# A one-column constant tile widened by 64 bytes in a two-layer hybrid attention kernel

## The chip, the cores and the metric

The kernel runs on one core of a Trainium2 chip. The metric is device microseconds of one execution. Before the change the median of 3 runs is 918.7 us, with runs from 918.14 to 919.21 us.

## The reference

A decoder trunk of two layers on x of 256 tokens by 1024 features, all in float32. Each layer has three sublayers, each followed by a layer norm of (alpha x + f(x)):

```
for l in range(DEPTH):
    y = hybrid_mixer(x, ...)                 # sparse, latent and forgetting attention, gated and merged
    x = layer_norm(DN_ALPHA * x + y, ...)
    y = memory_cross_attention(x, mem, ...)  # 4 heads into mem (256 rows)
    x = layer_norm(DN_ALPHA * x + y, ...)
    y = jnp.square(jax.nn.relu(x @ mlp_w_up[l])) @ mlp_w_down[l]
    x = layer_norm(DN_ALPHA * x + y, ...)
```

The weights are some 140 MB of float32, read once; nearly all the arithmetic is dense products of x, or of something made from x, with them.

## The kernel before

**Products in three passes.** Every dense product is made of float32r matmuls. A value v is split into hi = v rounded by ScalarE's write to float32r and lo = v - hi by VectorE. A product a b is then hi hi + lo hi + hi lo, accumulated in one PSUM bank. This is `mm3` (L317 to L325); its one matmul call is L322, so nearly all of TensorE's work carries that line, and groups are told apart by the tile names. In a row `mm<-xhi,whi` the first name after the arrow is the moving operand, the second the stationary one that the weight load brings in.

**Two shapes of product.** `f_tile` (L327) makes features on the partitions: the weights are stationary (128x128) and x moves (256 columns), 8 k-tiles by 3 passes, 24 matmuls per unit of weights. `t_chunk` (L579) makes tokens on the partitions: x is stationary and the weights move, mostly 512 columns at a time. In a layer, 65 units go through `f_tile` with x moving (misc, fq, fk, nq, ncv, nk, gmf, gn, up). With x stationary `t_chunk` takes 4 units each of t1, t2 and ut (48 matmuls of 512 columns each), and xq (48 of 256 columns). Other products have no x in them: the merged heads (`ofm`, `on`), the latent rows (`chi`, `clo`), the memory (`phi`, `plo` in the cross attention), the compressed windows (`xc`), the merged rows `mg` and the hidden layer `hh`, `hl`.

**The weight stream.** All weights lie in HBM in the order of use, as units of [128, 1024] float32. `load_to` (L242) has SyncE load each into one of 5 `raw` buffers; `split_piece` (L254) makes `whi`, `wlo` (6 buffers each) or, for t1, ut and mem, `phi`, `plo` in pages. `pump` (L272) is called from `tick` after a microsecond of products and splits a few units ahead.

**SBUF.** `run` (L1127) opens the pools in a fixed order: consts, small, raw, wp, pg (12 pages of 4096 bytes, 6 halves of 2048 bytes, both per partition), sp, pp. Each tile takes its bytes per partition, rounded up to 32, and the next begins behind it. `first_loads` (L356) allocates, in the order of the consts pool, `xhi` and `xlo` (8192 bytes each), then `mhalf` (one column of -0.5, for the power -1/2 on GpSimd), then `cst` and `ropek`. What comes later lies behind `mhalf`. Where the built program puts them, in bytes of a partition:

```
tile                       begins at    modulo 128
xhi, xlo                   16512, 24704      0
mhalf                      32896             0
cst                        32928            32
biasq, xtok                36576, 45792     96
raw (first of 5)           61248            64
whi, wlo (first of 6)      81728, 106304    64
halves (first of 6)        130880           64
pages (first of 12)        143168           64
sp and pp tiles            from 192320      64
```

The tiles of raw, whi, wlo, the halves, the pages, sp and pp lie multiples of 1024 bytes apart, and the slices that the dense products read begin at multiples of 512 bytes within their tile, so all of these have one remainder modulo 128.

Of the kernel before, what the change touches and what calls it, by code (L numbers as in the profile page):

```python
# [10 lines left out]
F32 = mybir.dt.float32  # L11
# [4 lines left out]
PSUM = bass.MemoryType.PSUM  # L16

S = 256
D = 1024
L = 2  # L20
P = 128
# [4 lines left out]
ROOT = 32.0  # of D  # L26
SPL = 512
# [14 lines left out]
RW0 = 271  # L42
# [24 lines left out]
def f_units(w, cols):  # L67
    """[K, n*128] columns -> n units of [128, K//128 * 128]."""
    k = w.shape[0] // P
    out = []  # L70
    for c in cols:
        sub = w[:, c] if not isinstance(c, slice) else w[:, c]
        out.append(sub.reshape(k, P, P).transpose(1, 0, 2).reshape(P, k * P))
    return out


def t_units(w, per):
    """[K, n] -> units of `per` k-tiles, [128, per * n]."""
    k = w.shape[0] // P
    a = w.reshape(k // per, per, P, w.shape[1]).transpose(0, 2, 1, 3)  # L80
    return [u.reshape(P, -1) for u in a]
# [106 lines left out]
class Halves:  # L188
    """Two tiles of four k-tiles, indexed as one."""
# [12 lines left out]
class Side:  # L202
    """Steps in order, each with the ticks to wait since the one before."""
# [26 lines left out]
class Kernel:  # L230
# [10 lines left out]
    # -- weights: load ahead, split each into hi + lo of 12 bits --  # L241
    def load_to(self, u):  # L242
        """Loads of the units up to u."""
        src = self.a["wst"]
        while self.next_load <= min(u, len(self.units) - 1):
            t = self.raw.tile([P, 1024], F32, name="raw", tag="raw")
            n = 512 if self.next_load == 0 else 1024
            for c in range(0, 1024, n):
                self.nc.sync.dma_start(t[:, c:c + n], bass.AP(
                    tensor=src.tensor, offset=src.offset + self.next_load * P * 1024 + c, ap=[[1024, P], [1, n]]))  # L250
            self.raws[self.next_load] = t
            self.next_load += 1

    def split_piece(self):  # L254
        """Splits the next SPL columns of the stream."""
        u, c = divmod(self.next_piece, 1024 // SPL)
        self.next_piece += 1
        self.load_to(u)
        if c == 0:
            if self.paged(u):  # L260
                self.halves[u] = (self.page([P, 1024], F32R, "phi"), self.page([P, 1024], F32R, "plo"))
            else:
                self.halves[u] = tuple(self.wp.tile([P, 1024], F32R, name=n, tag=n) for n in ("whi", "wlo"))
        sl = (slice(None), slice(c * SPL, c * SPL + SPL))
        hi, lo = self.halves[u]
        self.nc.scalar.activation(hi[sl], self.raws[u][sl], AF.Copy)  # L266
        self.nc.vector.tensor_sub(lo[sl], self.raws[u][sl], r(hi[sl]))  # L267
# [4 lines left out]
    def pump(self):  # L272
        """One piece ahead of use, as far as the buffers reach."""
        u = self.next_piece // (1024 // SPL)
        if u >= len(self.units):
            return
        used = self.offs[self.gi]
        ahead = sum(not self.paged(v) for v in range(used, u))
        if u - used < AHEAD_PAGED and (self.paged(u) or ahead < AHEAD):
            self.split_piece()  # L280
        self.load_to(self.next_piece // (1024 // SPL) + LOADS)
# [16 lines left out]
    # -- chains of steps that are emitted between the dense products --  # L298
    def tick(self, us):
        """After `us` of dense products on the tensor engine."""  # L300
        self.work += us
        while self.work >= TICK:
            self.work -= TICK
            for q in self.side:
                q.tick()
            self.pump()
# [8 lines left out]
    # -- products in three passes --  # L315
    def mm3(self, out, pairs, first=True, last=True):
        """pairs: ((lhs hi, lhs lo), (rhs hi, rhs lo)) accumulated in out."""  # L317
        mm = self.nc.tensor.matmul
        n = len(pairs)
        for ps, (i, j) in enumerate(((0, 0), (1, 0), (0, 1))):  # L320
            for k, (a, b) in enumerate(pairs):
                mm(out, a[i], b[j], start=first and ps == 0 and k == 0,  # L322
                   stop=last and ps == 2 and k == n - 1)
            self.tick(n * out.shape[-1] / 2400)
# [11 lines left out]
    def to_hilo(self, hi, lo, src, scale=None):  # L336
        """hi + lo = src * scale"""
        nc = self.nc
        if scale is None:
            nc.scalar.activation(hi, src, AF.Copy)  # L340
            nc.vector.tensor_sub(lo, src, r(hi))  # L341
        else:
            nc.scalar.activation(hi, src, AF.Copy, scale=scale)
            nc.vector.scalar_tensor_tensor(lo, src, scale, r(hi), op0=OP.mult, op1=OP.subtract)
# [10 lines left out]
    # -- set-up --  # L355
    def first_loads(self):  # L356
        nc, c, a = self.nc, self.consts, self.a
        # products of zeros, so that the tensor engine's clock is up when the first data come
        zero = self.half([P, 512], mybir.dt.bfloat16, "zero")
        nc.vector.memset(zero, 0.0)  # L360
        ps = self.bank("S", [P, 512])
# [14 lines left out]
        self.mhalf = c.tile([P, 1], F32, name="mhalf")  # L376
# [10 lines left out]
    def bias_tables(self):  # L387
        nc, c, a = self.nc, self.consts, self.a
# [5 lines left out]
        # the bias by distance, from -RW0 on; later read in skewed rows  # L394
        rs = self.page([8, RW], F32, "rs")
        for i in range(2):
            ps = self.bank("S", [P, 512])
# [4 lines left out]
    def bias_tables2(self):  # L402
# [3 lines left out]
        for q in range(4):  # L406
            # row p holds distances from p - RW0 on; keys run against them
# [34 lines left out]
    # -- x <- LayerNorm(alpha x + f); then its transposed halves --  # L442
    def ln_part(self, tb, i, ac, square=True):
        """z = alpha x + f for half a row, its sum, its mean square about the mean of the first half."""
# [20 lines left out]
    def layer_norm(self, tb, gb, final=False):  # L465
        """Adds the rest as steps."""
# [5 lines left out]
        def stats():  # L472
            z = st["z"] = self.page([P, D], F32, "lnz")
            # the variance is the mean square about the first half's mean less the square of the means' difference
# [29 lines left out]
    # -- attention over 64-wide heads, in pairs on the partitions --  # L504
    def probs(self, p_ap, s_ap, bias, sums, nmax):
        """p = exp(s + bias - max), its row sums"""
# [7 lines left out]
    def attend(self, qk, bias, v, kbs, done, apart=False):  # L514
        """Four heads with their own keys and values, as two chains of steps (logits to probabilities, the rest).
        qk(ps, h): the logits of head h; v(kb, h): values; done(o, pairs): o in PSUM, per pair of heads 128 columns;
        apart: one pair at a time."""
        nc = self.nc
        nk = P * len(kbs)
        # heads of one half of the partitions share a bank; sums in the order (parity, pair)  # L520
# [46 lines left out]
    def chain(self, units, q=0, wait=1.0):  # L567
        """Steps of units: the first chain of a unit between those of the second of the unit before."""
# [9 lines left out]
    def t_chunk(self, us, acc, x, per, n, tbs=(0, 1), tb_outer=True):  # L578
        """Token rows of x @ w for token blocks; unit u holds `per` k-tiles of n columns."""  # L579
# [8 lines left out]
    def mixer(self, l):  # L588
        nc, s = self.nc, self.small
        x = (self.xhi, self.xlo)  # L590
# [50 lines left out]
        # per head; row 64: 1 beside the keys' sums of -log f, row 65: the queries' sums of log f beside 1  # L641
# [8 lines left out]
        # gates and forget logits in token rows  # L650
# [8 lines left out]
        # -log sigmoid(z) = max(-z, 0) + log1p(exp(-|z|)), log1p(u) = 2 atanh(u / (2 + u))  # L659
# [21 lines left out]
        # selected / window values: [block, branch, group, hi | lo]  # L681
# [6 lines left out]
        # cumulative sums of -log f, turned into rows: [(block, head), token], + and -  # L688
# [75 lines left out]
        # windows of the compressed branch: [(parity, d), k-tile, keys | values, hi | lo, group, window]  # L764
# [21 lines left out]
        # keys of (selected, window): hi in both halves, lo beside the hi of q  # L786
# [42 lines left out]
        def cmp_keys():  # L829
            # in two halves like those above: hi (both halves), lo; per head a block of 16 of 64 columns  # L830
# [8 lines left out]
        def cmp_values():  # L839
            # block-diagonal over the heads of a group  # L840
# [172 lines left out]
    def cross(self, l):  # L1013
# [6 lines left out]
        # queries by token rows, so that the first block starts early; then transposed  # L1020
# [6 lines left out]
        for tb in range(2):  # L1027
# [21 lines left out]
            # weighted sums wait for the values  # L1049
# [31 lines left out]
    def mlp(self, l):  # L1081
# [3 lines left out]
        # the first four tiles of the hidden layer by token rows, one token block at a time  # L1085
# [86 lines left out]
```

## Time and profile before

| | |
|---|---|
| median of 3 runs | 918.7 us (918.14 to 919.21) |
| profiled execution: span from first to last instruction | 916.6 us |
| median run less that span (what lies around it; the profile gives no other time for its own execution) | 2.1 us |
| TensorE busy | 894.2 us, 98% of the span, 6062 matmuls |
| VectorE, ScalarE, GpSimd busy | 639.3, 540.3, 53.3 us |
| granted TensorE clock, mean | 0.997 of full |
| read from HBM | 158.68 MB, 174 GB/s over the span |

The page of a profile lists busy time by engine, the span in 40 slices, the DMA queues, the chain of work that ended last, and the costliest groups of instructions with the mean length of one. The length of one matmul covers its whole way through the array, and matmuls overlap: what one costs in a row of equal ones is the distance from a start to the next start, which the view of instructions in order of time gives. There equal neighbours are merged into one row, with the start of the first and their number.

### The profile page before, as it was taken

How to read it: one execution, taken by the hardware profiler on the slowest of the kernel's cores; microseconds unless marked ns; L12 is line 12 of the kernel's file. 1: busy time of each engine (PE TensorE's matmuls, PEld its weight loads, DVE VectorE, ACT ScalarE, POOL GpSimd, SP SyncE). 2: the span in 40 equal slices, each digit the busy share in tenths (PEclk: the TensorE clock that was granted, in tenths of full speed). 3: DMA queues.
4: the chain of work that ended last, by engine and by line, in shares of the span. 5: the costliest groups of instructions: out<-in, count | busy, mean ns of one | idle time of the engine just before them, and what ended most of it. 6: DMA issues, size and time to landing. Idle time of an engine off the chain costs nothing.

```text
span 916.6 us, 16139 instructions
## 1 busy us (share of the span) xinstructions
PE 894.2 (98%) x6062; PEld 800.2 (87%) x6062; DVE 639.3 (70%) x1401; ACT 540.3 (59%) x1167; POOL 53.3 (6%) x114
## 2 busy tenths in 40 slices
PE   8999999999999999999999999999999999999996
PEld 6899898998877999999888999889978689999995
DVE  5888787759886555555776988776678855555554
ACT  6777856556674555445655876665566644445551
POOL 1000000000211000000130000000021300000002
PEclk9999999999999999999999999999999999999998
DMA  8855544547463666656645445444567536665631
GB/s 324 264 178 156 199 141 139 159 139 274 145 224 128 194 184 185 186 195 193 207 129 170 142 137 183 139 138 138 143 249 232 173 132 194 188 186 189 190 104 46
DMA packets 46539, 160.80 MB, mean 175 GB/s; under 512 B 5941, under 2 KB 7381, under 8 KB 46334
## 3 DMA queue, kind: packets, MB, share of 16 engines
q1 hardware_dynamic: 46462, 159.78, 54.2%
q8 instruction: 47, 0.77, 0.3%
q14 instruction: 30, 0.25, 0.1%
HBM read 158.68 MB, written 1.07 MB: 174 GB/s over the span
## 4 chain that ended last, share of the span: by engine, by line
PE 87%; DVE 4%; POOL 3%; ACT 2%; issue 1%; DMA 1%; SPq 0%; DVEq 0%; POOLq 0%; ACTq 0%
PE mm L322 52%; PE S L322 13%; PE O L322 10%; PE S L903 1%; PE T L919 1%; POOL mv L476 1%; PE S L744 1%; PE S L1041 1%; DVE xtok L486 1%; PE O L944 1%; DVE xtok L450 1%; DVE wlo L267 1%; DVE xlo L341 1%; PE T L551 1%; PE O L561 1%
## 5 line engine op out<-in xcount | busy, mean ns | idle before, releaser
L267 DVE TENSOR_TENSOR wlo<-raw,whi 128x512 fp32r<-128x512 f32 x524 | 341.3, 687 | 119.0 <-ACT whi L266 115.2
L266 ACT ACTIVATE whi<-raw 128x512 fp32r<-128x512 f32 x524 | 302.9, 625 | 151.9 <-issue 98.4
L322 PE MATMUL mm<-xhi,whi 128*128 128x256 f32 x1024 | 144.9, 283 | 0.0
L322 PE MATMUL mm<-xlo,whi 128*128 128x256 f32 x1024 | 144.1, 282 | 0.0
L322 PE MATMUL mm<-xhi,wlo 128*128 128x256 f32 x1024 | 142.9, 281 | 0.0
L322 PEld LDWEIGHTS mm<-xhi,whi 128*128 128x128 f32 x1024 | 131.4, 188 | 5.4 <-issue 2.9
L322 PEld LDWEIGHTS mm<-xlo,whi 128*128 128x128 f32 x1024 | 130.2, 188 | 2.5 <-issue 0.5
L322 PEld LDWEIGHTS mm<-xhi,wlo 128*128 128x128 f32 x1024 | 130.0, 188 | 2.4 <-issue 1.3
L459 POOL TENSOR_SCALAR mv<-mv 128x1 f32<-128x1 f32 x36 | 9.1, 265 | 745.6 <-DVE xtok L450 744.6
L512 ACT ACTIVATE P<-sb,nm 128x128 f32<-128x128 f32 (+1 forms) x96 | 42.8, 447 | 16.0 <-DVE nm L510 15.8
L322 PE MATMUL S<-whi,hh 128*128 128x512 f32 x128 | 50.4, 394 | 0.0
L322 PE MATMUL S<-wlo,hh 128*128 128x512 f32 x128 | 50.1, 391 | 0.0
L322 PE MATMUL O<-whi,hh 128*128 128x512 f32 x128 | 50.0, 391 | 0.0
L322 PE MATMUL O<-wlo,hh 128*128 128x512 f32 x128 | 49.9, 390 | 0.0
L322 PE MATMUL O<-whi,hl 128*128 128x512 f32 x128 | 49.8, 389 | 0.0
L322 PE MATMUL S<-whi,hl 128*128 128x512 f32 x128 | 49.7, 389 | 0.0
L1116 DVE TENSOR_TENSOR tg<-tg 128x512 f32<-128x512 f32 x28 | 19.4, 693 | 38.7 <-ACT tg L1115 38.7
L1115 ACT ACTIVATE tg<-mm 128x512 f32<-128x512 f32 x28 | 16.7, 598 | 43.5 <-PE mm L322 43.5
L461 ACT ACTIVATE lnsq<-xtok,mv 128x512 f32<-128x512 f32 x24 | 17.3, 723 | 27.9 <-POOL mv L459 15.3
L267 DVE TENSOR_TENSOR plo<-raw,phi 128x512 fp32r<-128x512 f32 x40 | 25.9, 689 | 4.9 <-ACT phi L266 4.7
L322 PEld LDWEIGHTS S<-wlo,hh 128*128 128x128 f32 x128 | 24.0, 188 | 5.6
L322 PEld LDWEIGHTS O<-whi,hl 128*128 128x128 f32 x128 | 24.0, 188 | 5.1
(304 smaller groups left out, 1438.0 us busy)
## 6 DMA issues: line engine op xcount, KB each, us to landing
raw<-in_wst_dram SPq DMA_DIRECT2D x281, 512.0 KB, 3.7
lng<-in_lng_dram SPq DMA_DIRECT2D x6, 512.0 KB, 5.5
lnb<-in_lnb_dram SPq DMA_DIRECT2D x6, 512.0 KB, 5.8
wskew<-bias_scratch SPq DMA_DIRECT2D x4, 400.0 KB, 6.7
xt<-in_xT_dram SPq DMA_DIRECT2D x4, 256.0 KB, 4.2
xtok<-in_xtok_dram SPq DMA_DIRECT2D x1, 1024.0 KB, 5.6
out_dram<-xtok SPq DMA_DIRECT2D x4, 256.0 KB
raw<-in_wst_dram SPq DMA_DIRECT2D x2, 256.0 KB, 5.1
```

The costliest lines, as they stand in the source:

```text
L266: self.nc.scalar.activation(hi[sl], self.raws[u][sl], AF.Copy)
L267: self.nc.vector.tensor_sub(lo[sl], self.raws[u][sl], r(hi[sl]))
L322: mm(out, a[i], b[j], start=first and ps == 0 and k == 0, stop=last and ps == 2 and k == n - 1)
L341: nc.vector.tensor_sub(lo, src, r(hi))
L450: nc.vector.scalar_tensor_tensor(xs, xs, ALPHA, ac, op0=OP.mult, op1=OP.add, accum_out=mv[:, i:i + 1])
L461: nc.scalar.activation(sq, xs, AF.Square, bias=mv[:, 4:5], scale=1.0 / ROOT, accum_out=mv[:, 2 + i:3 + i])
L476: nc.gpsimd.tensor_scalar(col[9], col[8], col[8], col[7], op0=OP.mult, op1=OP.subtract)
L486: nc.vector.scalar_tensor_tensor(x[:, c], st["z"][:, c], col[11], gb[1][:, c], op0=OP.mult, op1=OP.add)
L512: nc.scalar.activation(p_ap, t[:, :n], AF.Exp, bias=nmax, scale=-1.0, accum_out=sums)
L551: nc.tensor.transpose(tp[:, h, :], pts[h % 2][:, h // 2, kb * P:(kb + 1) * P], self.ident)
L1115: nc.scalar.activation(t, ps, AF.Relu)
L1116: nc.vector.tensor_mul(t, t, t)
```

## The change

`mhalf` is allocated as 17 columns of which the first is used, 68 bytes for 4. With the rounding to 32 bytes, everything behind it in SBUF begins 64 bytes later. `xhi` and `xlo` lie ahead of it and stay. Comments are taken out elsewhere (their lines stay, blank), and a blank line is added here, so lines from 377 on count one higher. No instruction is added, removed or moved on any engine.

```diff
@@ -373,7 +373,8 @@
             if i % 2 == 0:
                 for _ in range(2 * 1024 // SPL):
                     self.split_piece()
-        self.mhalf = c.tile([P, 1], F32, name="mhalf")
+
+        self.mhalf = c.tile([P, 17], F32, name="mhalf")[:, 0:1]
         nc.vector.memset(self.mhalf, -0.5)
         self.load_to(6)
         self.cst = c.tile([P, K_END], F32, name="cst")
```

The built program's positions with the change, modulo 128: `xhi`, `xlo`, `mhalf` 0 (as before); `cst` 96; `biasq`, `xtok` 32; raw, whi, wlo, halves, pages, sp and pp tiles 0. Modulo 256, x begins at 128 in both; raw, whi, wlo and the pages at 64 before and at 128 with the change. Modulo 512, x begins at 128; whi, wlo and the pages at 320 before and at 384 with the change.

## Rows read from the trace of the kernel before

**Rows 1.** The page: busy time and instructions; granted clock of the 40 slices.

```profile
PE 894.2 (98%) x6062; PEld 800.2 (87%) x6062; DVE 639.3 (70%) x1401; ACT 540.3 (59%) x1167; POOL 53.3 (6%) x114
...
PEclk9999999999999999999999999999999999999998
```

**Rows 2.** The page: chain that ended last, shares of the span by engine.

```profile
PE 87%; DVE 4%; POOL 3%; ACT 2%; issue 1%; DMA 1%; SPq 0%; DVEq 0%; POOLq 0%; ACTq 0%
```

**Rows 3.** Groups by line and shape, TensorE: name, shape, count, busy us, mean ns.

```profile
L322 PE MATMUL mm<-xhi,whi 128*128 128x256 f32 x1024 | 144.9, 283 | 0.0
...
L322 PE MATMUL mm<-onhi,whi 128*128 128x256 f32 x64 | 10.3, 283 | 0.0
...
L322 PE MATMUL mm<-whi,xhi 128*128 128x512 f32 x32 | 10.3, 402 | 0.0
```

**Rows 4.** TensorE in order of time, 196.5 to 216 us: start, length, group.

```profile
198.39 1.10 PE L322 MATMUL mm<-xhi,wlo 128*128 128x256 f32 x8
199.34 1.10 PE L322 MATMUL mm<-xlo,whi 128*128 128x256 f32 x8
...
202.16 1.10 PE L322 MATMUL mm<-xlo,whi 128*128 128x256 f32 x8
...
203.59 0.64 PE L322 MATMUL mm<-onhi,wlo 128*128 128x256 f32 x4
...
214.15 0.64 PE L322 MATMUL mm<-onlo,whi 128*128 128x256 f32 x4
```

**Rows 5.** The same view, 476 to 500 us.

```profile
477.31 1.07 PE L322 MATMUL mm<-xhi,wlo 128*128 128x256 f32 x8
...
486.38 1.07 PE L322 MATMUL mm<-xlo,whi 128*128 128x256 f32 x8
...
488.65 0.63 PE L322 MATMUL mm<-wlo,xhi 128*128 128x512 f32 x2
...
498.45 0.62 PE L322 MATMUL mm<-wlo,xhi 128*128 128x512 f32 x2
```

**Rows 6.** The same view, 440 to 476 us: hidden layer by the weights of the down product.

```profile
446.09 0.39 PE L322 MATMUL S<-whi,hh 128*128 128x512 f32 x1
...
453.12 0.39 PE L322 MATMUL O<-whi,hl 128*128 128x512 f32 x1
```

**Rows 7.** The same view, 171 to 181 us: among steps of attention.

```profile
172.12 0.40 PE L322 MATMUL mm<-ofmhi,wlo 128*128 128x256 f32 x2
...
173.07 0.41 PE L322 MATMUL mm<-ofmlo,whi 128*128 128x256 f32 x2
...
175.16 1.07 PE L322 MATMUL mm<-xhi,wlo 128*128 128x256 f32 x8
176.07 1.07 PE L322 MATMUL mm<-xlo,whi 128*128 128x256 f32 x8
```

**Rows 8.** The same view, 69 to 73 and 632 to 637 us: first and last row of eight lasting 1.07 us.

```profile
71.58 1.07 PE L322 MATMUL mm<-xlo,whi 128*128 128x256 f32 x8
...
633.58 1.07 PE L322 MATMUL mm<-xhi,wlo 128*128 128x256 f32 x8
```

**Rows 9.** The same view, 245.9 to 253 us: queries of the cross attention, x stationary.

```profile
246.12 0.62 PE L322 MATMUL mm<-whi,xhi 128*128 128x256 f32 x4
...
248.84 0.62 PE L322 MATMUL mm<-whi,xhi 128*128 128x256 f32 x4
```

**Rows 10.** Groups by line and shape, ScalarE: the rounding that makes the upper halves.

```profile
L266 ACT ACTIVATE whi<-raw 128x512 fp32r<-128x512 f32 x524 | 302.9, 625 | 151.9 <-issue 98.4 <-PE mm L322 25.8 <-ACT hh L340 10.1
...
L340 ACT ACTIVATE xhi<-xt 128x512 fp32r<-128x512 f32 x4 | 2.4, 619 | 1.5 <-DMA xt<-in_xT_dram 1.5
```

**Rows 11.** Groups by line and shape, VectorE: the subtraction that makes the lower halves.

```profile
L267 DVE TENSOR_TENSOR wlo<-raw,whi 128x512 fp32r<-128x512 f32 x524 | 341.3, 687 | 119.0 <-ACT whi L266 115.2
...
L341 DVE TENSOR_TENSOR xlo<-xt,xhi 128x512 fp32r<-128x512 f32 x4 | 2.7, 686 | 1.4 <-ACT xhi L340 1.4
```

**Rows 12.** DMA issues: tile, count, KB each, median us from issue to landing.

```profile
raw<-in_wst_dram SPq DMA_DIRECT2D x281, 512.0 KB, 3.7
```

**Rows 13.** Chain that ended last, in order of time: its two longest DMA pieces.

```profile
2.10 6.19 DMA raw<-in_wst_dram
...
86.36 6.14 DMA wskew<-bias_scratch
```

## The prediction

> **What bounds the kernel now.** First the page's busy times: TensorE is busy for 894.2 of 916.6 us, VectorE for 70% and ScalarE for 59% [rows 1]. Then the chain that ended last: 87% of it is TensorE's, 1% DMA [rows 2]. [...] So the time is the sum of what the matmuls cost in a row, and a change that moves no instruction counts by what it does to that distance from start to start.
>
> The reader is then to see that the distance is not one number. [...] The groups by shape hide the difference (x and `on` as the moving operand both show a mean of 283 ns, the length of the whole way through the array [rows 3]). The view in order of time has it:
> - x moving, 256 columns: from 198.39 to 202.16 us are 32 starts, 117.8 ns each, 0.943 us per eight [rows 4]. That is the common, long step.
> - `on` moving, 256 columns, right behind it and with the same kind of stationary weights: from 203.59 to 214.15 us are 88 starts, 120.0 ns each [rows 4].
> - x moving again at 477.31 to 486.38 us: 80 starts, 113.4 ns each, 0.907 us per eight [rows 5]. A row of eight at this short step lasts 1.07 us, at the long one 1.10 us; I counted 41 short ones among the 390 rows of eight, the first at 71.58 us and the last at 633.58 us [rows 8].
> - x stationary, 256 columns: 246.12 to 248.84 us, 24 starts, 113.3 ns each [rows 9].
> - x stationary, 512 columns: 488.65 to 498.45 us, 42 starts, 233.3 ns each [rows 5].
> - no x, 512 columns: 446.09 to 453.12 us, 31 starts, 226.8 ns each [rows 6].
>
> Shape, dtype, line and pass structure are the same within each width. What goes with the step is whether x is one of the two operands. With x in the pair (one operand at 0 modulo 128, the other at 64) the step is 113 or 118 ns, whichever of the two x is, and 233 ns for 512 columns. Without x (both at 64) it is 120 and 227 ns. I read this as: the step depends on how the two operands' starts lie to each other, because moving the odd one from one operand to the other changes less than taking it away.
>
> **The change part by part.** Everything behind `mhalf` moves by 64 bytes together, so the places of weights, pages, halves and small tiles to each other stay. Only the places of `xhi` and `xlo` to the rest change: x and its partner now have equal remainders, as `on` and its weights have now. The terms:
>
> 1. *x moving, 256 columns.* 130 units (65 in each of 2 layers) by 24 matmuls are 3120, or 390 runs of eight. 82 units (misc, fq, fk, gn, up), 246 runs, stand in long rows: they go from 0.943 to 8 x 120.0 = 0.960 us, +0.017 each, +4.2 us. The other 48 units (nq, ncv, nk, gmf), 144 runs, are cut up by steps of attention. There `ofm` without x goes from 172.12 to 173.07 us in 8 starts, 118.8 ns each [rows 7], so a run goes from 0.943 to 0.950, +0.007, +1.0 us. The 41 runs with the short step have 0.036 us more to lose, +1.5 us. Together +6.7 us. The bounds: 0, if all run as those among attention, and +8.1 us, if all come to 120.0.
> 2. *x stationary, 512 columns.* t1, t2 and ut of 2 layers are 288 matmuls. From 233.3 to 226.8 ns is -6.5 ns each, -1.9 us. Bounds 0 and -1.9.
> 3. *x stationary, 256 columns.* xq, 96 matmuls, from 113.3 to 120.0 ns, +0.6 us. Bounds 0 and +0.6.
> 4. *Products without x*, some 740 of 256 and 1000 of 512 columns: both operands move alike, so I take 0. The short step bounds it at -4.9 us for the former (740 by 6.6 ns); that is priced in the first rival, and the other side in the last.
> 5. *ScalarE and VectorE.* Writing to x (at 0) where reading from 64 takes 619 and 686 ns, against 625 and 687 ns when both are at 64 [rows 10, 11]. Even 6 ns on the 564 pieces of the splits are 3 us of engines that wait for TensorE for longer than that; 0. That cover is gone only where TensorE waits for a split, and the chain has 4% of VectorE and 2% of ScalarE [rows 2]: 1% of 6% of 917 us is 0.5 us either way.
> 6. *DMA.* No row here has a load that lands at 0 modulo 128. A unit takes 3.7 us to land [rows 12] and five buffers stand ahead of use; on the chain are two long pieces, 6.19 and 6.14 us [rows 13]. A tenth more or less on both is 1.2 us either way; I take 0, since the order and sizes of all loads stay.
> 7. *`mhalf` itself.* The memset and the powers on GpSimd read and write the same one column; the chain's 3% of GpSimd stays.
>
> Sum: 6.7 - 1.9 + 0.6 = +5.4 us. On the profiled execution the span goes from 916.6 to 922.0 us. The median of the runs stands 2.1 us above that span, so I expect 924.1 us, and say **924 us**. With the bounds of the terms the forecast's own range is 921 to 928 us.
>
> [...]
>
> **The rivals.**
>
> *Faster: the next pairing is the free one.* The mechanism is that the two streams of reads meet at certain distances only, and that the distance x to weights repeats over more than 128 bytes. `on` and its weights lie 0 apart modulo 512; x and its weights will lie 256 apart, which no row shows. Then x's runs would all take the short step, 0.907 us: 349 runs by -0.036 are -12.6 us, with term 2 -14.5 us: **904 us**. If instead each operand's own start counted, the products without x would gain their 4.9 us too, 899 us. It decides wherever f_tile runs: 82 units would show rows of 1.07 us. For it: the short step exists with x and never in the long row of `on`. Against it: x as moving and x as stationary operand lie 64 and 192 apart modulo 256 and 320 and 192 modulo 512, and the pair shows the same short step, so the pattern looks like one of 128 bytes.
>
> *No change.* The step would come from something that goes with x but not from its address: its tile is 8192 bytes, and its chains are 8 long where those of `on` are 4. For it: the 113 and 118 ns steps both occur at unchanged addresses [rows 5, 7], so the address is not all. The mixed products, whose x-less rows are as long as x's, speak against it [rows 4, 6]. [...] **918.7 us**, 917 to 920.
>
> *Slower by more.* Products without x lose their good step of 512 columns: 1000 by 6.5 ns are +6.5 us, and term 2 gives nothing back, +1.9: **932 us**. Nothing in the trace asks for it.
>
> **How the numbers follow.** A difference under about 0.2% (1.8 us) can't be told from none. The forecast has a chance of 0.52, slower by more 0.04, no change 0.13, faster 0.31 (the distances 256 apart are seen in no row, so this stays large). Slower by over 0.2% then has 0.56, within 0.2% 0.13, faster 0.31. The range must reach from the forecast over no change into the faster case until 2 in 10 are out: up to 928, leaving out the slower rival, and down to 903, which takes in x's short step at 904 but not the larger gain at 899. Cases of both signs hold the most of it; the likeliest one's own range is 921 to 928.
>
> **What would show it.** In the changed kernel's view in order of time: rows of eight with x moving 0.960 us apart in the mlp and the gn stretch, pairs of t2 0.454 us apart instead of 0.467, `on` and the hidden layer as before, and fewer rows of 1.07 us. If rows with x come at 0.907 us, the first rival is right; if they stay at 0.943, the second. If t2 goes to 0.454 but x moving does not go to 0.960, places to each other count, but not as I read them. Any change in the idle time of ScalarE or VectorE before the splits larger than 3 us would make terms 5 and 6 wrong.

## The result and the profile after

The changed kernel takes 924.6 us (median of 4 runs, 924.43 to 925.72), against 918.45 us for the kernel before in the same comparison (4 runs): 1.0067 times as long, interval 1.0055 to 1.0078. Its profiled execution has a span of 923.9 us, 7.3 more than before.

The page shows first where the change does not act. Instruction counts, VectorE, ScalarE, GpSimd and the clock's slices are as in [rows 1], and the chain's shares are those of [rows 2] but for a point of ScalarE. Only TensorE's busy time, for matmuls and for weight loads, has grown.

```profile
PE 900.3 (97%) x6062; PEld 809.1 (88%) x6062; DVE 639.7 (69%) x1401; ACT 539.9 (58%) x1167; POOL 53.3 (6%) x114
...
PEclk9999999999999999999999999999999999999998
...
PE 87%; DVE 4%; ACT 3%; POOL 3%; DMA 1%; issue 1%; SPq 0%; DVEq 0%; POOLq 0%; ACTq 0%
```

TensorE in order of time after the change (start, length, group), the stretch of [rows 4]:

```profile
198.91 1.12 PE L322 MATMUL mm<-xlo,whi 128*128 128x256 f32 x8
199.87 1.12 PE L322 MATMUL mm<-xhi,whi 128*128 128x256 f32 x8
...
204.67 1.12 PE L322 MATMUL mm<-xlo,whi 128*128 128x256 f32 x8
...
206.11 0.64 PE L322 MATMUL mm<-onhi,wlo 128*128 128x256 f32 x4
...
216.67 0.64 PE L322 MATMUL mm<-onlo,whi 128*128 128x256 f32 x4
```

With x moving, 48 starts take 204.67 - 198.91 = 5.76 us, 120.0 ns each, where they took 117.8. `on` moving has 88 starts in 10.56 us, 120.0 ns as before. The stretch of [rows 5] had the short step:

```profile
481.06 1.12 PE L322 MATMUL mm<-xhi,wlo 128*128 128x256 f32 x8
...
490.65 1.12 PE L322 MATMUL mm<-xlo,whi 128*128 128x256 f32 x8
...
492.97 0.62 PE L322 MATMUL mm<-wlo,xhi 128*128 128x512 f32 x2
...
502.50 0.62 PE L322 MATMUL mm<-wlo,xhi 128*128 128x512 f32 x2
```

Now 80 starts take 9.59 us, 119.9 ns each, where they took 113.4. A row of eight lasts 1.12 us: the rows of 1.07 us [rows 8] are gone. The t2 product goes the other way: 42 starts in 9.53 us, 226.9 ns where it was 233.3. The two smaller stretches, xq [rows 9] and the hidden layer without x [rows 6], in the same view:

```profile
249.12 0.64 PE L322 MATMUL mm<-whi,xlo 128*128 128x256 f32 x4
...
251.52 0.64 PE L322 MATMUL mm<-whi,xhi 128*128 128x256 f32 x4
```

```profile
449.95 0.39 PE L322 MATMUL S<-whi,hh 128*128 128x512 f32 x1
...
456.75 0.39 PE L322 MATMUL O<-whi,hh 128*128 128x512 f32 x1
```

xq takes 2.40 us for 20 starts, 120.0 ns (113.3 before); the hidden layer 6.80 us for 30, 226.7 ns, as before. The groups by shape hide all of this again: the mean length of one matmul has moved by 3 ns [rows 3], and the two engines that make the splits are as in [rows 10, 11].

```profile
L267 DVE TENSOR_TENSOR wlo<-raw,whi 128x512 fp32r<-128x512 f32 x524 | 341.2, 686 | 121.4 <-ACT whi L266 118.0
L266 ACT ACTIVATE whi<-raw 128x512 fp32r<-128x512 f32 x524 | 302.5, 624 | 154.7 <-issue 99.7 <-PE mm L322 27.0 <-ACT hh L340 9.9
L322 PE MATMUL mm<-xhi,whi 128*128 128x256 f32 x1024 | 147.0, 286 | 0.0
```

For the whole execution I summed, over all matmuls of a class, the distance from each start to the next one on TensorE, whatever that is. A distance up to 150 ns (260 ns for 512 columns) counts for the mean step; longer ones are joints, where TensorE went over to other work or waited.

| class | matmuls | sum before, us | sum after, us | difference | step before, ns | step after, ns |
|---|---|---|---|---|---|---|
| x moving, 256 columns | 3120 | 377.3 | 385.0 | +7.6 | 117.4 | 119.8 |
| x stationary, 512 columns | 288 | 73.9 | 73.0 | -1.0 | 233.3 | 227.8 |
| x stationary, 256 columns (xq) | 96 | 11.6 | 12.0 | +0.4 | 114.7 | 119.5 |
| no x, 256 columns | 724 | 92.8 | 92.8 | 0.0 | 119.7 | 119.6 |
| no x, 512 columns, most by `hh` or `hl`, the rest by `mg` and the heads of the cross attention | 1007 | 236.6 | 236.3 | -0.3 | 228.0 | 227.8 |

Together +6.9 of the span's +7.3 us (differences and their total are from unrounded sums). The classes with x carry it; those without hardly move.

### The profile page after: what moved, and what is told of

It is laid out like the page before. It is cut to its first block, busy times and chain, and to the rows that moved or that the text cites. A ratio compares the mean times of both kernels' runs of the same rounds, so it can differ in the third digit from the quotient of the medians.

```text
span 923.9 us, 16139 instructions
## 1 busy us (share of the span) xinstructions
PE 900.3 (97%) x6062; PEld 809.1 (88%) x6062; DVE 639.7 (69%) x1401; ACT 539.9 (58%) x1167; POOL 53.3 (6%) x114
## 3 DMA queue, kind: packets, MB, share of 16 engines
HBM read 158.68 MB, written 1.07 MB: 173 GB/s over the span
## 4 chain that ended last, share of the span: by engine, by line
PE 87%; DVE 4%; ACT 3%; POOL 3%; DMA 1%; issue 1%; SPq 0%; DVEq 0%; POOLq 0%; ACTq 0%
PE mm L322 52%; PE S L322 14%; PE O L322 10%; PE S L904 1%; PE T L920 1%; PE S L745 1%; PE S L1042 1%; POOL mv L477 1%; DVE xtok L487 1%; PE O L945 1%; DMA wskew<-bias_scratch 1%; DVE xtok L451 1%; ACT whi L266 1%; DVE wlo L267 1%; PE T L552 1%
## 5 line engine op out<-in xcount | busy, mean ns | idle before, releaser
L322 PE MATMUL mm<-xhi,whi 128*128 128x256 f32 x1024 | 147.0, 286 | 0.0
L322 PE MATMUL mm<-xlo,whi 128*128 128x256 f32 x1024 | 146.9, 286 | 0.0
L322 PE MATMUL mm<-xhi,wlo 128*128 128x256 f32 x1024 | 145.6, 285 | 0.0
L322 PEld LDWEIGHTS mm<-xhi,whi 128*128 128x128 f32 x1024 | 133.4, 191 | 5.4 <-issue 2.8
L322 PEld LDWEIGHTS mm<-xlo,whi 128*128 128x128 f32 x1024 | 132.9, 191 | 2.4 <-issue 0.5
L322 PEld LDWEIGHTS mm<-xhi,wlo 128*128 128x128 f32 x1024 | 132.6, 191 | 2.4 <-issue 1.3
L322 PEld LDWEIGHTS O<-whi,hh 128*128 128x128 f32 x128 | 24.0, 188 | 5.0
```

Of the source, the lines that this page charges most:

```text
L322: mm(out, a[i], b[j], start=first and ps == 0 and k == 0, stop=last and ps == 2 and k == n - 1)
```

## The experiments

That x's rows got longer does not yet say why. Three theories stood against each other. **Distance**: the step follows from where the two operands' starts lie to each other, modulo some power of two. **Own start**: it follows from where each operand begins, whatever its partner, so that a start at 0 modulo 128 would be bad or good by itself. **No address**: it goes with x's tile or its chains of eight. All runs are compared with the kernel before on the same chip (918.9 to 919.3 us). "Distance" below is the start of weights, pages and halves less that of x, modulo 128: 64 before, 0 with the change.

**x moved along with the rest.** The change is kept, and x is moved by 64 bytes too, so that the old relation of starts is gone but none of these operands begins at a multiple of 128.

```diff
-        self.xhi = c.tile([P, KT, S], F32R, name="xhi")
+        self.xhi = c.tile([P, KT * S + 16], F32R, name="xhi")[:, 16:].rearrange("p (k s) -> p k s", k=KT)
-        self.mhalf = c.tile([P, 1], F32, name="mhalf")
+        self.mhalf = c.tile([P, 17], F32, name="mhalf")[:, 0:1]
```

> x is moved to 64 modulo 128 as well (16 columns ahead of xhi's data) and mhalf is widened as in the change, so that x and the weights have equal remainders again, both 64 instead of both 0. If the places of the two operands to each other count: as the changed kernel, 924 to 925 us, x moving at 120 ns a step in long rows, t2 at 227 ns. If each operand's own start at a multiple of 128 counts: another time, and x-less products unlike those of the changed kernel.

Measured: 925.64 us, 1.0063 times before (1.0045 to 1.0082). Its TensorE in order of time:

```profile
480.51 1.12 PE L322 MATMUL mm<-xhi,wlo 128*128 128x256 f32 x8
...
490.11 1.12 PE L322 MATMUL mm<-xlo,whi 128*128 128x256 f32 x8
...
492.43 0.62 PE L322 MATMUL mm<-wlo,xhi 128*128 128x512 f32 x2
...
501.96 0.62 PE L322 MATMUL mm<-wlo,xhi 128*128 128x512 f32 x2
```

80 starts in 9.60 us, 120.0 ns; 42 in 9.53 us, 226.9 ns. These are the changed kernel's steps, with both operands at 64 instead of 0.

**Weights at 0, x at 64.** The same edit to `xhi`, but `mhalf` as before. Everything behind x then begins where the change puts it, and x moves away from it.

```diff
-        self.xhi = c.tile([P, KT, S], F32R, name="xhi")
+        self.xhi = c.tile([P, KT * S + 16], F32R, name="xhi")[:, 16:].rearrange("p (k s) -> p k s", k=KT)
```

> x is moved to 64 modulo 128 and all the rest comes to 0, which is the changed kernel's place for weights, pages and halves, with x off by 64. If places to each other count: as before the change, 918 to 919 us, x moving at 118 ns with some rows at 113, t2 at 233 ns. If weights, pages and halves at multiples of 128 cost the time: as the change, 924 to 925 us.

Measured: 919.52 us, ratio 1.0000 (0.9990 to 1.0011). TensorE in order of time:

```profile
198.65 1.10 PE L322 MATMUL mm<-xhi,wlo 128*128 128x256 f32 x8
...
202.42 1.10 PE L322 MATMUL mm<-xlo,whi 128*128 128x256 f32 x8
...
203.84 0.64 PE L322 MATMUL mm<-onhi,wlo 128*128 128x256 f32 x4
...
214.40 0.64 PE L322 MATMUL mm<-onlo,whi 128*128 128x256 f32 x4
```

```profile
479.46 1.07 PE L322 MATMUL mm<-xhi,whi 128*128 128x256 f32 x8
...
486.72 1.07 PE L322 MATMUL mm<-xlo,whi 128*128 128x256 f32 x8
...
488.99 0.63 PE L322 MATMUL mm<-wlo,xhi 128*128 128x512 f32 x2
...
498.79 0.62 PE L322 MATMUL mm<-wlo,xhi 128*128 128x512 f32 x2
```

x moving takes 117.8 ns in the first stretch (32 starts in 3.77 us) and 113.4 ns in the second (64 in 7.26 us), t2 233.3 ns, `on` 120.0 ns: in these stretches the kernel before, step for step, with every weight at the address that the change gives it. (Over the execution too, but for the 96 matmuls of xq: 115.9 ns, where they took 114.7.) The two runs together are a crossed test, and both leave only the distance standing: equal starts cost what the change costs wherever they lie, and starts 64 apart cost what the kernel before costs wherever they lie. Own start and no address fall.

**Other distances.** `mhalf` with 9 columns puts weights, pages and halves at 96, with 25 at 32.

```diff
-        self.mhalf = c.tile([P, 1], F32, name="mhalf")
+        self.mhalf = c.tile([P, 9], F32, name="mhalf")[:, 0:1]
```

> mhalf widened by 32 bytes: x at 0, the rest at 96 modulo 128. A distance of x to the rest that no run has had yet. If the distance counts: a step of its own for x, between 113.4 and 120 ns for 256 columns, 904 to 926 us; products without x as before (120 and 227 ns). If only the distance 0 is special: 918 to 919 us.

> mhalf widened by 96 bytes: x at 0, the rest at 32 modulo 128. As for the run before, with the distance on the other side; if the distance counts by its size alone, the same time as with 96. The two runs together also tell whether some distance gives x the short step of 113.4 ns throughout, which would be 904 us or less.

Measured: at 96, 917.43 us, 0.9978 (0.9967 to 0.9990), mean step with x moving 117.0 ns; at 32, 922.1 us, 1.0030 (1.0020 to 1.0039), mean step 118.3 ns. t2 and its like stay at 233 ns in both. The same stretches of the run at 96:

```profile
198.22 1.10 PE L322 MATMUL mm<-xlo,whi 128*128 128x256 f32 x8
...
203.87 1.10 PE L322 MATMUL mm<-xlo,whi 128*128 128x256 f32 x8
```

```profile
478.28 1.10 PE L322 MATMUL mm<-xhi,wlo 128*128 128x256 f32 x8
...
487.61 1.10 PE L322 MATMUL mm<-xlo,whi 128*128 128x256 f32 x8
```

117.7 ns and 116.6 ns: the common step is a little shorter than before, and the short one of 113 ns is no longer there. So 96 gains where 64 was long and loses where 64 was short; on the mean of the steps 0.4 ns for each of 3120 matmuls, 1.2 us. The profiled execution does not show that as a gain: it was, at 918.93 us, the longest of its ten, and the joints of x moving took 2.0 us more than before. Several distances thus have steps of their own: it is not a matter of hit or miss. Nor does the size of the distance alone decide: 32 and 96 are equally far from 0 modulo 128, on its two sides, and differ in time and step.

**x off by 16, 8 and 24 bytes.** Both x tiles get 4, 2 or 6 columns in front, to go below the 32 bytes to which tiles are rounded.

```diff
-        self.xhi = c.tile([P, KT, S], F32R, name="xhi")
-        self.xlo = c.tile([P, KT, S], F32R, name="xlo")
+        self.xhi = c.tile([P, KT * S + 2], F32R, name="xhi")[:, 2:].rearrange("p (k s) -> p k s", k=KT)
+        self.xlo = c.tile([P, KT * S + 2], F32R, name="xlo")[:, 2:].rearrange("p (k s) -> p k s", k=KT)
```

> One kernel, two finer distances: weights behind xhi by 112 and behind xlo by 80 modulo 128 (measured so far for both: 0 gives 119.8 ns a step of 256 columns, 96 gives 117.0, 64 gives 117.4, 32 gives 118.3, means without the joints). If the step changes smoothly with the distance: xhi at 118 to 119 ns, xlo at 117 to 117.5, and a time of 918 to 921 us. If something between 64 and 128 is free of the cost: one of them near 113.4 ns, and under 915 us.

> Distances 120 for xhi and 88 for xlo. Smooth: xhi at 119 to 120 ns, xlo at 117, 919 to 922 us. A distance that is free of the cost: 113.4 ns.

> Distances 104 for xhi and 72 for xlo. Smooth: both at 117 to 117.6 ns, 917 to 919 us. A distance that is free of the cost: 113.4 ns.

Measured: off by 16 (distances 112 for `xhi`, 80 for `xlo`), 920.69 us, 1.0016 (1.0006 to 1.0027), steps 117.9 and 118.4 ns. That is not the smooth course that was expected: 80 lies between 64 and 96 and steps longer than both. Off by 8, 945.81 us, 1.0294 (1.0273 to 1.0314); off by 24, 947.12 us, 1.0308 (1.0287 to 1.0329). The last two have another reason for most of their time. TensorE and its transposes of x behind the cross attention's layer norm, off by 8, in order of time (in brackets the idle time before and what ended it):

```profile
278.51 0.40 PE L322 MATMUL mm<-plo,xhi 128*128 128x512 f32 x1
284.55 1.94 PE L492 MATMUL T<-cst,xtok 128*128 128x128 f32 x8 [5.64 <-DVE xtok L486]
286.38 0.79 PE L322 MATMUL mm<-plo,xhi 128*128 128x512 f32 x1
286.97 1.05 PE L322 MATMUL mm<-phi,xhi 128*128 128x512 f32 x2
287.82 1.05 PE L322 MATMUL mm<-phi,xlo 128*128 128x512 f32 x2
```

In the kernel before, the 24 products of `phi` and `plo` with the first token block's x all run ahead of the second block's transposes:

```profile
274.38 0.50 PE L322 MATMUL mm<-phi,xhi 128*128 128x512 f32 x1
...
280.21 0.63 PE L322 MATMUL mm<-plo,xhi 128*128 128x512 f32 x2
282.04 1.29 PE L492 MATMUL T<-cst,xtok 128*128 128x128 f32 x8 [1.21 <-DVE xtok L486]
```

With x off by 8 only five of the 24 do, the last at 278.51 us; the others come behind those transposes. TensorE stands idle for 5.64 us, and after that the granted clock between 284 and 290 us is 0.58 on the mean: the first products run at 425 ns from start to start (0.85 us for two), and from 289.31 us on at 230; between 290 and 296 us the granted clock is 1.00. Two more idle stretches, of 4.29 and 5.63 us, stand ahead of the transposes of two later layer norms, and TensorE's idle time in all goes from 13.8 to 26.3 us. Over the execution, the class with x stationary and 512 columns grows by 14.7 us. In both programs (off by 8 and by 24) TensorE's instructions stand in another order than before, and ScalarE's writes of `xhi` from the transposes have 32 waits where they had 22; in every other run of this document TensorE's order is that of the kernel before. So the edit changed the program, not only an address. What stays usable is the step in long rows that wait for nothing:

```profile
30.32 1.12 PE L322 MATMUL mm<-xlo,whi 128*128 128x256 f32 x8
...
33.20 1.12 PE L322 MATMUL mm<-xlo,whi 128*128 128x256 f32 x8
```

That is 120.0 ns (24 starts in 2.88 us), at a distance of 120 from `xhi` and 88 from `xlo`, and the same with 104 and 72. Over the execution the mean is 120.1 ns in both runs; at 64, 80, 96 and 112 it was 117.0 to 118.4. So an x that begins 8 bytes off a multiple of 16 runs at the long step at all four distances. As the weights lie at 0 in both runs, these distances are 8 modulo 16 too; whether x's own start or the distance does it is not separated.

**The best distance for both kinds of product.** Weights and halves at 96 from x, and the pages, in which `on`, `ofm` and the other moving operands without x lie, back at 0, so that those are 96 from the weights as well. The halves get a pool of their own ahead of the pages, and a gap of 32 bytes.

```diff
-        return self.pg.tile(shape, dt, name=name, tag="hp", bufs=self.NHALF)
+        return self.hp.tile(shape, dt, name=name, tag="hp")
...
-        self.mhalf = c.tile([P, 1], F32, name="mhalf")
+        self.mhalf = c.tile([P, 9], F32, name="mhalf")[:, 0:1]
...
+            self.hp = en(tc.tile_pool(name="hp", bufs=self.NHALF))
+            self.gap = en(tc.tile_pool(name="gap", bufs=1)).tile([P, 8], F32, name="gap")
```

> Weights and halves at 96 modulo 128 as in the run with 96, pages at 0 like x (the halves have a pool of their own, with 32 bytes between it and the pages). If the distance of the two operands sets every step: t1 and ut (192 matmuls of 512 columns) come from 233 to 228 ns, -1.0 us; the products of pages as moving operand with whi, wlo (on, ofm, chi, mem, some 700) come from 119.5 to 117 ns, -1.7 us; mg with the weights (192) goes from 227 to 233, +1.2 us. Together -1.5 us on the run with 96: some 916 us. If the distance counts for x alone: 917.4 us as there.

Measured: 916.95 us, 0.9975 times before (0.9965 to 0.9985), where the changed kernel stands at 1.0067. That is the lowest ratio of all that was run, but the run at 96 (0.9978, from 0.9967 to 0.9990) can't be told from it, where 1.5 us less had been forecast. The products without x, `on` at 120.0 ns in the runs above, now have another step:

```profile
204.59 0.63 PE L322 MATMUL mm<-onhi,wlo 128*128 128x256 f32 x4
...
214.86 0.63 PE L322 MATMUL mm<-onlo,whi 128*128 128x256 f32 x4
```

88 starts in 10.27 us, 116.7 ns instead of 120.0. Their class goes from 92.8 to 91.3 us, that with x moving from 377.3 to 376.6. So `on` had been at the long step since its page and its weights lay at the same place modulo 128, as the prediction supposed, and not because of its shorter chains.

The same run crosses the products of 512 columns as well. t1 and ut, whose weights lie in pages and so come back to 0 from x, step at 228.1 ns (233.3 before), while t2, whose weights stay at 96, has 233.2. The merged rows `mg`, which lie in pages, now are 96 from their weights and lose the good step. Before, and then in this run:

```profile
216.01 1.07 PE L322 MATMUL S<-whi,mg 128*128 128x512 f32 x4
...
224.17 1.07 PE L322 MATMUL S<-whi,mg 128*128 128x512 f32 x4
```

```profile
216.73 1.09 PE L322 MATMUL S<-whi,mg 128*128 128x512 f32 x4
...
225.13 1.09 PE L322 MATMUL S<-whi,mg 128*128 128x512 f32 x4
```

36 starts in 8.16 us are 226.7 ns, in 8.40 us 233.3; over the execution the 192 matmuls by `mg` take 0.9 us more. Products with no x in them thus gain or lose by the distance of their own two operands: it is not x's tile, nor the place of x to the tiles that the other engines write, that sets the step.

**How long the pattern is.** x moved by other means, so that x and weights both lie at 64 modulo 128, but 128 apart modulo 256. `cst` and `t5` are allocated ahead of `xhi`; loads and order stay.

```diff
+        self.cst = c.tile([P, K_END], F32, name="cst")
+        self.t5 = c.tile([33, 8], F32, name="t5")
         self.xhi = c.tile([P, KT, S], F32R, name="xhi")
...
-        self.cst = c.tile([P, K_END], F32, name="cst")
...
-        t5 = c.tile([33, 8], F32, name="t5")
+        t5 = self.t5
```

> cst and t5 are allocated ahead of xhi, mhalf is as before: everything behind stays where it was before the change, x moves to 64 modulo 128 and lies 128 from the weights modulo 256 (0 modulo 128). So far every pair that is 0 apart modulo 128 was also 0 apart modulo 256. If the pattern repeats every 128 bytes: x moving at 120 ns in long rows, t2 at 227 ns, 924 to 926 us. If it repeats every 256 or more: another step, and a time between 904 and 922 us.

Measured: 924.86 us, 1.0061 (1.0044 to 1.0078). The time alone is the change's, but the steps are not:

```profile
198.29 1.13 PE L322 MATMUL mm<-xlo,whi 128*128 128x256 f32 x8
...
204.06 1.13 PE L322 MATMUL mm<-xlo,whi 128*128 128x256 f32 x8
```

```profile
480.72 1.12 PE L322 MATMUL mm<-xhi,wlo 128*128 128x256 f32 x8
...
490.22 1.11 PE L322 MATMUL mm<-xlo,whi 128*128 128x256 f32 x8
...
492.52 0.64 PE L322 MATMUL mm<-wlo,xhi 128*128 128x512 f32 x2
...
502.28 0.63 PE L322 MATMUL mm<-wlo,xhi 128*128 128x512 f32 x2
```

The first stretch has the change's step to within the rows' rounding (48 starts in 5.77 us, 120.2 ns, against 120.0), the second 118.8 ns where the change has 119.9; over the execution most single steps spread from 115 to 123 ns with a mean of 119.3. t2 stays at 232.4 ns, where equal starts give 226.9. Two starts 128 apart are therefore not the same as two starts 0 apart: the pattern is longer than 128 bytes, and that the times agree is a coincidence of a smaller loss with x moving and no gain with x stationary. Whether it repeats after 256 bytes was tried only so far as the change itself tells: its x and weights lie 256 apart modulo 512, `on` and its weights 0 apart, and both take 120.0 ns; and in the run with pages at 0, x lies 224 from its weights modulo 512 and `on` 480, and both take 116.7 ns in their long rows.

This bears on the distances above, which are given modulo 128. Modulo 256 they are those of the second column: 64, 80, 96 and 112 were all tried on one side only, and nothing was tried between 32 and 128 or between 128 and 192.

The steps in one table (mean of all matmuls with x moving, without joints; the time against before on the same chip):

| distance modulo 128 | modulo 256 | x moving, 256 columns, ns | x stationary, 512 columns, ns | time against before |
|---|---|---|---|---|
| 0 (the change) | 0 | 119.8 | 227.8 | 1.0067 |
| 0 (x and weights at 64) | 0 | 119.8 | 227.9 | 1.0063 |
| 32 | 32 | 118.3 | 233.2 | 1.0030 |
| 64 (x at 64, weights at 0) | 192 | 117.4 | 233.2 | 1.0000 |
| 64 (before) | 192 | 117.4 | 233.3 | 1 |
| 80 and 112 (x off by 16) | 208 and 240 | 118.4, 117.9 | 229.8 | 1.0016 |
| 96 | 224 | 117.0 | 233.1 | 0.9978 |
| 0 (x moved by 2624 bytes) | 128 | 119.3 | 232.7 | 1.0061 |

## Why the prediction was right

The forecast of 924 us stands 0.6 us under the median of 924.6, and its mechanism, that the place of the two operands to each other sets the step, is the one that the crossed runs left standing (1.0063 and 1.0000 times before). By its terms:

1. *x moving.* Forecast +6.7 us, measured +7.6, inside the bounds of 0 and 8.1. The long rows came at the 0.960 us per eight that `on` gave (5.76 us for six). What was mis-sized is the part among steps of attention: `ofm` was taken as its measure, at 118.8 ns [rows 7], but the 48 units there came to a mean of 119.7 ns, and grew by 2.9 us of the 7.6 (forecast: 1.0, and 0.5 for their 15 of the 41 short rows), the other 82 by 4.7. Eight starts of `ofm` in one stretch, in rows rounded to 0.01 us, were too few to measure a step by: over the execution before, `ofm` has 119.3 ns.
2. *x stationary, 512 columns.* Forecast -1.9, measured -1.0. The step fell nearly as forecast, from 233.3 to 227.8 ns on the mean, 1.6 us for all 288; joints took back the rest.
3. *xq.* Forecast +0.6, measured +0.4, since outside the stretch of [rows 9] it had not all been at the short step (mean 114.7 ns before).
4. *Products without x.* Forecast 0; 92.8 us both times for 256 columns, -0.3 us for 512. The run with pages at 0 showed that this was a matter of distance too.
5. *ScalarE and VectorE.* Forecast 0; a split takes 624 and 686 ns, as before, and the idle time before the splits changed by less than 3 us on each.
6. *DMA.* Forecast 0 within 1.2 us. The chain in order of time has this:

```profile
1.17 4.64 DMA xt<-in_xT_dram
...
87.50 8.01 DMA wskew<-bias_scratch
```

The first piece is another load than in [rows 13], and shorter; the skewed read took 1.9 us longer. It shows no cost: from 500 to 750 matmuls into the program, the stretch that has this read, the changed kernel falls behind by 0.76 us, and the class with x moving accounts for 0.80 there. Nor does it go with the address: on the chain the read takes 6.34 us where x moves along, 5.86 at 32, 8.09 at 96.
7. *`mhalf`.* GpSimd 53.3 us both times.

The sum forecast for the span was +5.4; it is +7.3, and terms 1 and 2 hold the difference: 0.9 us more lost and 0.9 us less given back. The median is closer to its forecast than the span because the profiled execution, at 925.72 us, was the longest of the four, 1.1 us above the median; that closeness is luck.

Two things in the working do not come out. The bound of 0 for term 1, "if all run as those among attention", is not 0: 390 runs at 0.007 us are 2.7 us. The forecast's own range of 921 to 928 us does not come from the bounds: with term 1 at 0, term 2 at -1.9 and the rest at 0 the sum is 916.8 us, and the upper bounds of all terms come to 929.1.

The rivals. *The next pairing is free* fell: no row with x came at 0.907 us in the changed kernel. Its reason, a pattern longer than 128 bytes, was right all the same, and the prediction's argument for one of 128 was wrong (the run 128 apart modulo 256); that the new pairing, 256 apart modulo 512, behaves as 0 apart was seen in no row beforehand, and here the prediction had luck. The rival's version by own starts fell in the crossed runs. *No change* fell with them: the step does come from the address, and starts at multiples of 16 are not all alike: for the same work at other distances the runs give 117.0 to 119.8 ns for 256 columns, and 227.8 to 233.3 ns for 512. *Slower by more* fell: the products without x kept their step (119.7 and 119.6 ns for 256 columns, 228.0 and 227.8 for 512).

What stays open is the mechanism. That the reads of the moving operand and of the next weights meet in SBUF at some distances is an argument from the table, shown by no row. Open as well is why the same remainders give 113 ns in one stretch and 118 in another [rows 4, 5]; no run was made on that, and no distance tried gave 113 ns throughout. The kernel before shows that it is not the kind of unit: fq and fk step at 117.7 to 117.8 ns in the first layer and at 113.3 in the second. The step is also not one function of distance for both shapes: equal starts are the worst for 256 columns among starts at multiples of 16 (119.8 ns), and the best tried for 512 (227.8 ns).

## What to carry to other kernels

Where TensorE is busy throughout, read the distance from start to start by operand pair, not the mean length of a matmul: equal shapes that step differently at one clock (117.8 and 120.0 ns in the stretch of [rows 4], at a granted clock of 1.00) point to something other than arithmetic, here the place of the two operands to each other (119.8 ns with the change, 117.4 before). Starting the tiles of the dense products at multiples of 128 bytes put operands that are multiplied at equal remainders, the slowest choice tried for 256 columns moving among starts at multiples of 16 (119.8 ns against 117.0 to 119.3), and the best for 512 (227.8 against 229.8 to 233.3). Where 256 columns make up most of the time, try different remainders for tiles that are multiplied together, and test the claim crossed, by moving both and by moving only the other. A few tenths of a per cent hung here on a constant's width alone (`mhalf` with 9, 25 and 17 columns: 0.9978, 1.0030 and 1.0067 times before), so an edit that shifts SBUF by accident must be told apart from what it was meant to do.

## What the runs showed that was not expected

- The step for 256 moving columns has more than two values over the distance of the operands modulo 128: 119.8 ns at 0, 118.3 at 32, 117.4 at 64, 118.4 at 80, 117.0 at 96, 117.9 at 112. For 512 columns it is 227.8 at 0 and 233 at 32, 64 and 96, the other way round.
- Starts 128 apart modulo 256 are neither like 0 (t2 at 232.4 and not 226.9 ns) nor like 64 (118.8 ns, not 113.4, in the second stretch).
- An x that begins at 8 modulo 16 bytes steps at 120 ns at each of the four distances tried (72, 88, 104, 120).
- Slices of a tile that begin 8 or 24 bytes into it cost more through the program than through the address: with x off by 8 bytes the steps with x moving, 120.1 ns where they were 117.4, come to an estimated 8.4 us over 3120 matmuls, of 26.8 us in all, while 19 of the 24 products of one token block no longer ran before the transposes of the other, TensorE was idle for 5.64 us in one place, the granted clock was 0.58 over 6 us behind it, and the whole took 2.9% longer.
